# Narrower products for the diagonal key block in the two causal attentions of a hybrid decoder layer

## Chip, cores, metric

The kernel runs on one core of one Trainium2 chip. The metric is the device time of one execution in microseconds (us), the median of several runs. The engines are named as in the profile: PE (TensorE, products), PEld (its loads of the stationary operand, recorded apart), DVE (VectorE), ACT (ScalarE), POOL (GpSimd), SP (SyncE, which issues most transfers).

## What is computed

One decoder layer on 1024 tokens of width 1024: three mixers side by side (sparse attention A, latent attention B, cross-attention M into 256 memory tokens), each multiplied by a gate path, projected, merged by sigmoid gates and projected once more. What matters here are A and B, eight heads each, both causal over query blocks of 128:

```python
def one_block(args):                       # branch B; A is alike, with a top-k mask beside the causal one
    qb, start = args
    q_pos = start + jnp.arange(Q_BLOCK)    # Q_BLOCK = 128
    sc = jnp.einsum('bqhd,bkhd->bhqk', qb, k).astype(jnp.float32) * scale
    sc = jnp.where((key_pos[None, :] <= q_pos[:, None])[None, None], sc, NEG)
    p = jax.nn.softmax(sc, axis=-1).astype(v.dtype)
    return jnp.einsum('bhqk,bkhd->bqhd', p, v)
```

## The kernel before, in words

Every product of weight is made with float32r operands, a four-byte type that holds a rounded float32. To keep precision an operand is split in a high and a low part (names that end in h and l, as `b_3th` and `b_3tl`), and a product is two or three products of parts that add up in one bank of PSUM. Transposes go through PE as well, against an identity: `ident` for float32 data, `identr` for float32r data.

Both attentions run through the same function `attention`. Its work is cut into units of one head and one group G of two query blocks, 2G and 2G + 1, in the order G = 3, 0, 2, 1; there are 32 units in each branch. While the scores of one unit are made (`s_mm`, lines 997 to 999 in B with three products for each chunk of keys, 1481 and 1482 in A with two), the probabilities of the unit before it are multiplied with the values by class `PV`. For each pair of key blocks kp, `PV.pt` makes four transposes of 128x128 (line 466) into one bank, a cast by ACT to the high part (468) and a subtraction by DVE for the low part (469). `PV.mmv` then makes four products (479 and 480): values of key block 2kp against the high and the low part, and values of key block 2kp + 1 against both. Each streams 256 columns: the two query blocks side by side. `PV.evac` empties the result by ACT (487) and DVE (488).

The last pair, kp = G, holds the diagonal. Query block 2G sees nothing of key block 2G + 1, so only three of four 128x128 pieces are live. The kernel before keeps 256 columns there too: tiles `zt` hold zeros in their first quarter, written once by POOL at the start of each branch (441), and the other three quarters are filled by the casts. There are two pairs of such tiles in branch B (`ZTB`) and one in branch A. The other pairs use `pth` and `ptl` with two buffers each (`PVB`, `PVA`).

The first query block sees 128 keys, but `s_chunks` makes its scores 256 wide; the second half of the columns is not read.

Between these pieces stand products of other parts: the next pair of heads (`kv` in B, `a` in A) and the merge gates (`f`, class `Filler`), a few at a time by the counts in `PFB`, `PFA`, `GENB` and `GENA`. All of it is recorded in program order and then put into each engine's order by the framework's scheduler, which sees dependencies, buffers and pools. Where a size or a buffer changes, the order of rows on PE, ACT and DVE can change with it.

Of the kernel before, what the change touches and what calls it, by code (L numbers as in the profile page):

```python
# [73 lines left out]
ZTB = 2  # L74
PVB = (2, 2)
PVA = (2, 2)
# [28 lines left out]
def f(ap):  # L105
    return ap.bitcast(F32)
# [3 lines left out]
def hybrid_kernel(  # L110
# [32 lines left out]
    def ps_turn(nm, banks):  # L143
        """a bank of one of several kinds, in turn"""
        turn[0] += 1
        return banks[turn[0] % len(banks)](nm)

# [33 lines left out]
    # rotary tables: cos / sin of f32(position) * f32(inv_freq), by token block  # L181
# [40 lines left out]
    # DRAM scratch  # L222
# [30 lines left out]
    def wload(pool, nm, srcs, a, n):  # L253
        """srcs: list of ([128, a, w] DRAM view, w); -> (hi, lo) [P, a, n]"""
        def tile(dt, tag, bufs, nm):
            if len(pool_raw) < 3:
                return pool.tile([P, a, n], dt, tag=tag, name=nm, bufs=bufs)
            t = pool.tile([P, pool_raw[2]], dt, tag=tag, name=nm, bufs=bufs)
            return t[:, 0:a * n].rearrange("p (a n) -> p a n", a=a)
        raw = tile(F32, "raw", pool_raw[0], nm + "r")  # L260
        o = 0
        for ap, w in srcs:
            nc.sync.dma_start(raw[:, :, o:o + w], ap)
            o += w
        hi = tile(FR, "wp", pool_raw[1], nm + "h")
        lo = tile(FR, "wp", pool_raw[1], nm + "l")
        wsplit(hi, lo, raw)
        return hi, lo
# [12 lines left out]
    def proj_w(nm, pool, w, cols, nk, per=None):  # L281
        """cols: list of (c0, n) -> one (hi, lo) for each 128 rows"""
        tot = sum(n for _, n in cols)
        ks = []
        for kp in range(nk // 2):
            if per is not None:
                per(kp)
            hi, lo = wload(pool, f"{nm}w{kp}", [(wview(w, 2 * kp, 2, c0, n), n) for c0, n in cols], 2, tot)
            ks += [(hi[:, i, :], lo[:, i, :]) for i in range(2)]
        return ks  # L290

    def proj(nm, ks, lhs, tbs, chunks, consume):
        """out[tok, cols]; chunks: list of (off, n) within the columns"""
        nk = len(ks)
        for tb in tbs:
            for ci, (off, n) in enumerate(chunks):
                ps = ps_turn(f"{nm}ps{tb}_{ci}", pjb[0])
                for kt in range(nk):
                    ah, al = lhs(kt, tb)
                    wh, wl = ks[kt]  # L300
                    mm3(ps[:, 0:n], ah, al, wh[:, off:off + n], wl[:, off:off + n], kt == 0, kt == nk - 1)
                consume(tb, ci, ps)

# [15 lines left out]
    def row_factor(xp, xt, nm, r):  # L319
        """r <- rsqrt(mean square) of each row"""  # L320
        junk = xp.tile([P, D], BF, tag="junk", name=nm + "j", bufs=1)
        ss = sm.tile([P, 1], F32, tag="xss", name=nm + "ss")
        nc.scalar.activation(junk, xt, AF.Square, accum_out=ss)
        rsqrt_mean(r, ss, 1.0 / D)

    def norm_T(xp, xs, tbs, gcol, dst, nm, scale=True):
        """dst(k) -> (hi, lo) tiles [P, len(tbs) * 128]"""
# [16 lines left out]
    gates_done = set()  # L344

    class Filler:
        """tanh(gate / 2) of (branch, column block) jobs, a few products at a time"""
# [64 lines left out]
    def s_chunks(n):  # L412
        """(first key, width of the product, width used) of each bank"""
        if n <= 512:
            return [(0, max(n, 256), n)]
        if n == 640:
            return [(0, 384, 384), (384, 256, 256)]
        return [(0, 512, 512), (512, n - 512, n - 512)]
# [14 lines left out]
    zt = []  # L433
    zcount = [0]
    pv_bufs = [2, 2]

    def zero_tiles(wk, n):
        zt[:] = [[wk.tile([P, 4, P], FR, name=f"zt{i}{j}", bufs=1) for j in range(2)] for i in range(n)]
        for t2 in zt:
            for t in t2:  # L440
                nc.gpsimd.memset(t[:, 0, :].bitcast(F32), 0.0)

    class PV:
        """P of two query blocks (2G, 2G + 1) times V, transposed; vst(kt): [128, 128], high and low
        parts of V, the high part where the head's rows of the result lie."""
# [7 lines left out]
        def pt(self, kp):  # L453
            nm, wk, Pt = self.nm, self.wk, self.Pt
            tp = ps_t(f"{nm}pt{kp}").rearrange("p (a c) -> p a c", a=4)
            last = kp == self.nk - 1
            if last:
                th, tl = zt[zcount[0] % len(zt)]
                zcount[0] += 1
                order = [(1, 2 * kp + 1, 1), (2, 2 * kp, 0), (3, 2 * kp, 1)]  # L460
            else:
                th = wk.tile([P, 4, P], FR, tag="pth", name=f"{nm}th{kp}", bufs=pv_bufs[0])
                tl = wk.tile([P, 4, P], FR, tag="ptl", name=f"{nm}tl{kp}", bufs=pv_bufs[0])
                order = [(2 * a + b, 2 * kp + a, b) for a in range(2) for b in range(2)]
            for i, kt, b in order:
                nc.tensor.transpose(tp[:, i, :], Pt[b][:, kt * P:(kt + 1) * P], ident)
            v = slice(1 if last else 0, 4)
            nc.scalar.copy(th[:, v, :], tp[:, v, :])
            nc.vector.tensor_tensor(tl[:, v, :], tp[:, v, :], f(th[:, v, :]), op=ALU.subtract)
            kts = (2 * kp + 1, 2 * kp) if last else (2 * kp, 2 * kp + 1)  # L470
            self.t[kp] = (th.rearrange("p (a b) c -> p a (b c)", a=2), tl.rearrange("p (a b) c -> p a (b c)", a=2), kts)

        def mmv(self, kp):
            if self.o2 is None:
                self.o2 = ps_mm(f"{self.nm}o2")
            th, tl, kts = self.t.pop(kp)
            for a in range(2):
                vs = self.vst(kts[a])
                nc.tensor.matmul(self.o2[:, 0:256], vs, th[:, a], start=(kp == 0 and a == 0), stop=False)
                nc.tensor.matmul(self.o2[:, 0:256], vs, tl[:, a], start=False,  # L480
                                 stop=(kp == self.nk - 1 and a == 1))
# [10 lines left out]
    def masked(pt, sp, m, mask, k0, mx, c):  # L492
        """-(scores + mask), and its least value"""
# [40 lines left out]
    def attention(gen, k_prep, q_prep, scores, pv, fill, per, pre, GEN):  # L534
        """Head pairs; the next pair's operands are made between the units of this one."""
# [21 lines left out]
        def fl(k):  # L557
            """work of the next pair, then gate products"""
# [54 lines left out]
    # ================= memory branch =================  # L613
# [6 lines left out]
    with ExitStack() as ph:  # L620
# [31 lines left out]
        with ExitStack() as ph2:  # L652
# [44 lines left out]
            # the second half of h^T has no values yet: its tiles hold the weights of V  # L697
# [9 lines left out]
            # k_rope of branch B comes along with q_m  # L707
# [88 lines left out]
    # ================= branch B: latent attention =================  # L796
# [5 lines left out]
    def latent(nm, wpool, c0, nct, gofs, dst, wk, rb, rank, mid=None):  # L802
        """dst[ci] -> (hi, lo) [P, S]; what it returns sets rb to rsqrt(mean square) per token"""
# [19 lines left out]
        # three bfloat16 parts carry every bit of the sums  # L823
# [16 lines left out]
    with ExitStack() as ph:  # L840
        cb = ph.enter_context(tc.tile_pool(name="ckv", bufs=1, reuse_waits="tile"))
        ckv = [(cb.tile([P, S], FR, name=f"ckvh{i}"), cb.tile([P, S], FR, name=f"ckvl{i}")) for i in range(2)]
        with ExitStack() as ph2:
# [17 lines left out]
            # q_b = c_q w_uq: gain, rope; the norm's factor goes into the softmax scale  # L861
# [31 lines left out]
            # shared rotary key: sum of squares, gain, rotation  # L893
# [11 lines left out]
        zero_tiles(wk, ZTB)  # L905
# [118 lines left out]
    def topk_group(ts, nm, act):  # L1024
        """0 on the 256 largest of each row (the first ones among equals), NEG elsewhere: the bits of the
        256th largest value are found from the top by counting. VectorE counts values >= T. ScalarE sums
        the signs of x - T: (> T) - (< T), which may also settle on the number just below the 256th largest
        value when several values are equal to it; then the least value > T is the one."""
# [23 lines left out]
        # T has the low 16 bits all alike while its high half is sought: there the high halves of the values  # L1052
        # compare as the values do
# [5 lines left out]
        # on ScalarE T is kept negated  # L1059
# [19 lines left out]
        def sign(i, t):  # L1079
            """sign of x - T, and the number of positive ones"""  # L1080
# [51 lines left out]
    def both():  # L1132
        """steps of the two groups, TKR of VectorE's to one of ScalarE's"""
# [29 lines left out]
    if True:  # L1163
        pool_raw[:] = [2, 8]
        # ================= lightning indexer =================
# [74 lines left out]
    # ================= gates and branch projections =================  # L1240
    z_done = set()

    def z_part(n, w, zc, wpool, wk, zb=2, loaded=None):
        """2 silu(z) of 128 columns, by halves of the tokens"""
# [35 lines left out]
    def branch(n, zc, wpool, wk, yp, o_T, emit, bg=None, tgb=2, wkt=None, zb=2, ob=2, mid=None):  # L1280
        """emit(d, j, prod-writer) ; accumulates 4 * gate_n * branch_n transposed"""
# [86 lines left out]
    # ================= branch A: sparse attention =================  # L1368
    with w3s as ph:
# [17 lines left out]
        zero_tiles(wk2, 1)  # L1387
# [118 lines left out]
    # ================= branch A projection, merge, output projection =================  # L1506
# [91 lines left out]
```

## Time and profile before

| | us |
|---|---|
| median of 3 runs | 1428.13 |
| the runs | 1425.39 to 1431.31 |
| the profiled execution, its span | 1427.6 |

The profiled execution's own time is its span from the first to the last instruction; its runs lie around it on both sides, and the median is 0.5 us above it. In the rows below a line such as `L479` is a line of the kernel, `out<-in` are tile names with the numbers of buffers left out, and `128*128 128x256` means a stationary operand of 128x128 and 128 rows by 256 streamed columns. Starts in a timeline are rounded to 0.01 us. The recorded duration of a product holds its way through the array too, so consecutive records overlap; the pace is read from the starts.

### The profile page before, as it was taken

Reading aid. Unit: us, or ns where it says so; the run is one execution under the profiler, and the core shown is the slowest. Engines: PE = TensorE matmul, PEld = TensorE weight load, DVE = VectorE, ACT = ScalarE, POOL = GpSimd, SP = SyncE. Lnnn points to the kernel's source line nnn. Section 1 sums busy time; section 2 is a strip of 40 time slices with the busy share of each in tenths; the row PEclk is TensorE's granted clock in tenths of the full one; section 3 lists DMA queues with packets and bytes.
Section 4 is the critical chain, followed back from the end, with each engine's and each line's share of the span. In section 5 each row is a group of like instructions: output and inputs, shape, how many; then the busy total and the mean of one; then the engine's idle time right before and its main releaser. Section 6 shows DMA issues by size and latency. Waiting matters only on the chain.

```text
span 1427.6 us, 20798 instructions
## 1 busy us (share of the span) xinstructions
PE 1366.2 (96%) x7440; PEld 1173.0 (82%) x7440; DVE 967.5 (68%) x2409; ACT 687.7 (48%) x1488; POOL 270.2 (19%) x254
## 2 busy tenths in 40 slices
PE   7999999999999999898988998899999999999998
PEld 5998888888888889786867886689899898877887
DVE  5935446678888861479879678777777868836511
ACT  6635433356666651464576563224555535633200
POOL 3150003511102000200232335331202011003200
PEclk9999999999999999999998999999999999999999
DMA  7411222311111120210224325630201001185622
GB/s 245 136 45 52 78 59 86 114 56 41 49 56 53 45 93 20 67 45 23 89 79 151 97 75 182 193 85 9 67 23 45 31 15 45 38 276 184 210 96 74
DMA packets 124631, 122.34 MB, mean 86 GB/s; under 512 B 20336, under 2 KB 90224, under 8 KB 124528
## 3 DMA queue, kind: packets, MB, share of 16 engines
q1 hardware_dynamic: 123952, 118.92, 26.8%
q10 hardware_dynamic: 576, 2.10, 0.4%
q8 instruction: 58, 0.95, 0.3%
q14 instruction: 45, 0.37, 0.1%
HBM read 87.93 MB, written 33.06 MB: 85 GB/s over the span
## 4 chain that ended last, share of the span: by engine, by line
PE 68%; DVE 15%; ACT 6%; issue 4%; DMA 4%; POOL 1%; SPq 1%; ACTq 0%; DVEq 0%; POOLq 0%
PE f L277 5%; PE f L278 5%; PE f L279 4%; DVE kdj L1039 3%; PE a L277 3%; PE a L278 3%; PE a L279 3%; PE o L277 2%; PE o L278 2%; PE o L279 2%; ACT kag L1049 2%; PE br L277 2%; PE br L278 2%; PE br L279 2%; DVE sz L1292 1%
## 5 line engine op out<-in xcount | busy, mean ns | idle before, releaser
L1049 ACT ACTIVATE kag<-idx,kaT 128x512 bf16<-128x512 f32 (+2 forms) x96 | 82.9, 864 | 56.0 <-DVE kaT L1077 39.4
L277 PE MATMUL f<-hTh,f_0h 128*128 128x512 f32 x184 | 77.0, 419 | 1.9 <-ACT f_0h L248 1.2
L277 PE MATMUL f<-hTh,f_1h 128*128 128x512 f32 x184 | 75.6, 411 | 1.3 <-ACT f_1h L248 1.3
L279 PE MATMUL f<-hTh,f_0l 128*128 128x512 f32 x184 | 74.4, 405 | 0.6 <-POOL f_0l L251 0.6
L278 PE MATMUL f<-hTl,f_0h 128*128 128x512 f32 x184 | 74.5, 405 | 0.0
L279 PE MATMUL f<-hTh,f_1l 128*128 128x512 f32 x184 | 74.0, 402 | 0.0
L278 PE MATMUL f<-hTl,f_1h 128*128 128x512 f32 x184 | 73.6, 400 | 0.0
L1568 DVE TENSOR_TENSOR xr<-o,xr 128x512 f32<-128x512 f32 x16 | 11.1, 691 | 64.0 <-PE o L279 64.0
L1223 ACT ACTIVATE irl<-is 128x512 f32<-128x512 f32 (+1 forms) x80 | 37.6, 524 | 24.2 <-DVE idx L1229 15.5
L1526 POOL TENSOR_TENSOR ac<-ac,tg 128x512 f32<-128x512 f32 x16 | 23.5, 1469 | 128.6 <-DMA wo_3r<-in_w_out_dram 109.9
L1039 DVE TENSOR_SCALAR_CACHE_REDUCE kdj<-kdh,kdT 128x384 bf16<-128x384 bf16 (+2 forms) x48 | 46.3, 965 | 0.8
L1039 DVE TENSOR_SCALAR_CACHE_REDUCE kdj<-idx,kdT 128x384 bf16<-128x384 f32 (+2 forms) x48 | 46.2, 963 | 0.6
L369 ACT ACTIVATE fo<-f 128x512 f32<-128x512 f32 x48 | 28.7, 599 | 35.2 <-PE f L279 29.0
L279 PEld LDWEIGHTS f<-hTh,f_0l 128*128 128x128 f32 x184 | 35.2, 191 | 7.9 <-POOL f_0l L251 1.1
L1229 DVE SCALAR_TENSOR_TENSOR idx<-irl,wi,idx 128x1024 f32<-128x1024 f32 (+5 forms) x42 | 40.6, 966 | 1.5 <-ACT irl L1223 0.4
L277 PEld LDWEIGHTS f<-hTh,f_0h 128*128 128x128 f32 x184 | 35.1, 191 | 7.2 <-ACT f_0h L248 1.4
L279 PEld LDWEIGHTS f<-hTh,f_1l 128*128 128x128 f32 x184 | 34.8, 189 | 7.0 <-DVE f_1l L251 0.6
L277 PEld LDWEIGHTS f<-hTh,f_1h 128*128 128x128 f32 x184 | 35.0, 190 | 6.7 <-ACT f_1h L248 2.1
L278 PEld LDWEIGHTS f<-hTl,f_1h 128*128 128x128 f32 x184 | 34.9, 190 | 5.2
L278 PEld LDWEIGHTS f<-hTl,f_0h 128*128 128x128 f32 x184 | 35.3, 192 | 4.3
L1412 ACT ACTIVATE asq<-a 128x256 f32<-128x256 f32 x32 | 12.3, 384 | 51.1 <-PE a L279 50.9
L1266 DVE SCALAR_TENSOR_TENSOR sz<-sz,z 128x512 f32<-128x512 f32 x24 | 16.4, 683 | 27.7 <-ACT sz L1265 27.7
(1215 smaller groups left out, 4862.1 us busy)
## 6 DMA issues: line engine op xcount, KB each, us to landing
s_tg<-fo SPq DMA_DIRECT2D x48, 256.0 KB, 2.0
tg<-s_tg SPq DMA_DIRECT2D x48, 256.0 KB, 3.0
f_0r<-in_w_in_dram SPq DMA_DIRECT2D x23, 256.0 KB, 3.0
f_1r<-in_w_in_dram SPq DMA_DIRECT2D x23, 256.0 KB, 2.9
xx<-in_x_dram SPq DMA_DIRECT2D x8, 512.0 KB, 7.3
osb<-s_o SPq DMA_DIRECT2D x8, 512.0 KB, 3.8
s_acc<-acc SPq DMA_DIRECT2D x16, 256.0 KB, 2.4
ac<-s_acc SPq DMA_DIRECT2D x16, 256.0 KB, 3.4
```

The lines of the kernel that those rows point to most:

```text
L277: nc.tensor.matmul(ps, ah, bh, start=start, stop=False)
L278: nc.tensor.matmul(ps, ah, bl, start=False, stop=False)
L279: nc.tensor.matmul(ps, al, bh, start=False, stop=stop)
L369: nc.scalar.activation(o, ps, AF.Tanh, scale=0.5)
L1039: nc.vector.tensor_scalar(out=junk, in0=src[t], scalar1=T[:, i:i + 1], scalar2=0.0, op0=op, op1=ALU.add, accum_out=cnt[:, i:i + 1])
L1049: nc.scalar.activation(junk, idx[t], AF.Sign, bias=T[:, i:i + 1], accum_out=cnt[:, i:i + 1])
L1223: nc.scalar.activation(rl[:, k0:k0 + m], sp[:, 0:m], AF.Relu)
L1229: i_ = nc.vector.scalar_tensor_tensor(out=acc[:, 0:n], in0=rl[:, 0:n], scalar=wc, in1=acc[:, 0:n], op0=ALU.mult, op1=ALU.add)
L1266: zi[0] = nc.vector.scalar_tensor_tensor(out=sz, in0=sz, scalar=1.0, in1=pz[j], op0=ALU.add, op1=ALU.mult)
L1292: i_ = (nc.gpsimd if n and PMUL else nc.vector).tensor_tensor(sz, osb[:, cs], sz, op=ALU.mult)
L1412: nc.scalar.activation(sq.rearrange("p h d -> p (h d)"), ps[:, 0:256], AF.Square)
L1526: nc.gpsimd.tensor_tensor(ac, ac, tg, op=ALU.add)
```

## The change

The last pair of key blocks gets tiles of `pth` and `ptl` like the others, with the three live pieces side by side. The products with key block 2G keep 256 columns; those with key block 2G + 1 stream 128 columns into the second half of the result. The `zt` tiles and their memsets go, and `pth` and `ptl` get a third buffer. The scores of the first query block are 128 wide. The lines of comments that the diff also drops are left out here.

```diff
-ZTB = 2
-PVB = (2, 2)
-PVA = (2, 2)
+PVB = (3, 2)
+PVA = (3, 2)
...
     def s_chunks(n):
         if n <= 512:
-            return [(0, max(n, 256), n)]
+            return [(0, n, n)]
...
             last = kp == self.nk - 1
-            if last:
-                th, tl = zt[zcount[0] % len(zt)]
-                zcount[0] += 1
-                order = [(1, 2 * kp + 1, 1), (2, 2 * kp, 0), (3, 2 * kp, 1)]
-            else:
-                th = wk.tile([P, 4, P], FR, tag="pth", name=f"{nm}th{kp}", bufs=pv_bufs[0])
-                tl = wk.tile([P, 4, P], FR, tag="ptl", name=f"{nm}tl{kp}", bufs=pv_bufs[0])
-                order = [(2 * a + b, 2 * kp + a, b) for a in range(2) for b in range(2)]
-            for i, kt, b in order:
+            th = wk.tile([P, 4, P], FR, tag="pth", name=f"{nm}th{kp}", bufs=pv_bufs[0])
+            tl = wk.tile([P, 4, P], FR, tag="ptl", name=f"{nm}tl{kp}", bufs=pv_bufs[0])
+            order = [(2 * kp + a, b) for a in range(2) for b in range(2) if not (last and a > b)]
+            v = len(order)
+            for i, (kt, b) in enumerate(order):
                 nc.tensor.transpose(tp[:, i, :], Pt[b][:, kt * P:(kt + 1) * P], ident)
-            v = slice(1 if last else 0, 4)
...
         def mmv(self, kp):
...
             for a in range(2):
-                vs = self.vst(kts[a])
-                nc.tensor.matmul(self.o2[:, 0:256], vs, th[:, a], start=(kp == 0 and a == 0), stop=False)
-                nc.tensor.matmul(self.o2[:, 0:256], vs, tl[:, a], start=False,
-                                 stop=(kp == self.nk - 1 and a == 1))
+                vs = self.vst(2 * kp + a)
+                o = slice(P, 256) if last and a else slice(0, 256)
+                c = slice(256 * a, 256 * a + o.stop - o.start)
+                nc.tensor.matmul(self.o2[:, o], vs, th[:, c], start=(kp == 0 and a == 0), stop=False)
+                nc.tensor.matmul(self.o2[:, o], vs, tl[:, c], start=False, stop=bool(last and a))
...
-        zero_tiles(wk, ZTB)
...
-        zero_tiles(wk2, 1)
```

How the built order shows it, first on PE, at the end of the products of the first unit of branch B with its values (`b_3o` is that result, `b_2q` and `b_2S` belong to the next scores). Before:

```order
1643 L480 MATMUL b_3o_3228<-b_3tl_3221,vst_2885 128x256
1644 L479 MATMUL b_3o_3228<-b_3th_3220,vst_2885 128x256
1645 L480 MATMUL b_3o_3228<-b_3tl_3221,vst_2885 128x256
1646 L479 MATMUL b_3o_3228<-zt_2862,vst_2885 128x256
1647 L480 MATMUL b_3o_3228<-zt_2863,vst_2885 128x256
1648 L479 MATMUL b_3o_3228<-zt_2862,vst_2885 128x256
1649 L480 MATMUL b_3o_3228<-zt_2863,vst_2885 128x256
1650 L997 MATMUL b_2S_0_3273<-bkh_3009,b_2qh 128x384
```

The same place in the change, whose lines are some 11 to 13 lower:

```order
1639 L469 MATMUL b_3o_3220<-b_3tl_3213,vst_2877 128x256
1640 L966 MATMUL b_2q<-ident,xqp_2999 96x128 x2
1641 L468 MATMUL b_3o_3220<-b_3th_3226,vst_2877 128x256
1642 L469 MATMUL b_3o_3220<-b_3tl_3227,vst_2877 128x256
1643 L468 MATMUL b_3o_3220<-b_3th_3226,vst_2877 128x128
1644 L469 MATMUL b_3o_3220<-b_3tl_3227,vst_2877 128x128
1645 L984 MATMUL b_2S_0_3267<-bkh_3001,b_2qh 128x384
```

The number of products is the same, four; the last two are half as wide, and the first two no longer hold zeros. Rows of `kv` that stood ahead of them have moved behind.

On ACT, in branch A, where the probabilities of a unit with G = 3 are cast while the weights of the next pair of heads (`a3w0h`, `a3w1h`) are split. Before:

```order
994 L468 CAST a_3th_11768<-a_3pt_11767 128x512
995 L1418 CAST avst_11144<-a_6_11679 128x2x64
996 L248 CAST a3w0h<-a3w0r 128x768
997 L248 CAST a3w1h<-a3w1r 128x768
998 L468 CAST a_3th_11786<-a_3pt_11785 128x512
999 L468 CAST zt_9740<-a_3pt_11815 128x384
```

In the change:

```order
993 L455 CAST a_3th_11844<-a_3pt_11843 128x512
994 L501 ACTIVATE a_0p_11838,a_0rs<-a_0p_11838,a_0mx_11837 128x256
995 L1404 CAST avst_11212<-a_6_11755 128x2x64
996 L455 CAST a_3th_11862<-a_3pt_11861 128x512
997 L247 CAST a3w0h<-a3w0r 128x768
998 L247 CAST a3w1h<-a3w1r 128x768
999 L455 CAST a_3th_11892<-a_3pt_11891 128x384
```

The third cast, which has its own buffer now, stands ahead of the two casts of weights.

## Rows read from the trace of the kernel before

**Rows 1.** The page: span, and busy time of each engine.

```profile
span 1427.6 us, 20798 instructions
...
PE 1366.2 (96%) x7440; PEld 1173.0 (82%) x7440; DVE 967.5 (68%) x2409; ACT 687.7 (48%) x1488; POOL 270.2 (19%) x254
```

**Rows 2.** Busy time by stage, the columns named in the first line.

```profile
core 0: us, PE busy (x) PEld busy (x) DVE busy (x) ACT busy (x) POOL busy (x), PEclk, DMA share, GB/s
285.00:530.00 245.00, 241.70 (x1510) 210.33 (x1511) 198.59 (x582) 153.63 (x370) 25.58 (x29) 0.99 0.18 53
960.00:1250.00 290.00, 284.95 (x1745) 258.69 (x1746) 228.74 (x713) 153.49 (x364) 34.22 (x29) 0.99 0.12 35
```

**Rows 3.** What PE waited for, 285 to 530, then 960 to 1250, longest.

```profile
PE bkt L967 <- POOL xk L952: 2.4, 1, 2.4
...
PE akt L1449 <- DVE akd L1444: 2.9, 1, 2.9
```

**Rows 4.** Busy time by stage of instructions that touch `zt`.

```profile
285.00:530.00 245.00, 21.11 (x128) 19.09 (x128) 17.62 (x32) 15.42 (x32) 0.00 (x0) 0.99 0.18 53
960.00:1250.00 290.00, 22.39 (x128) 19.14 (x128) 17.58 (x32) 15.44 (x32) 0.00 (x0) 0.99 0.12 35
```

**Rows 5.** Readers of the first group's scores, `b_0S` and `a_0S`.

```profile
L494 DVE CUSTOM_DVE_ANT_0 b_0p<-b_0S,cmb x16: 273/351/420, 301.5 to 503.9; 128x128 f32<-128x128 f32 x8, 128x256 f32<-128x256 f32 x8
...
L494 DVE CUSTOM_DVE_ANT_0 a_0p<-a_0S,msk x16: 273/349/425, 973.2 to 1228.2; 128x128 f32<-128x128 f32 x8, 128x256 f32<-128x256 f32 x8
```

**Rows 6.** Timeline of PE, branch B: start us, us, engine, line, operation.

```profile
307.81 0.28 PE L479 MATMUL b_3o<-zt,vst 128*128 128x256 f32 x1
...
308.28 0.34 PE L997 MATMUL b_2S<-bkh,b_2qh 96*128 96x384 f32 x1
```

**Rows 7.** Timeline of PE, output projection: first and last of 22 rows.

```profile
1344.98 0.39 PE L277 MATMUL o<-wo_3h,hTh 128*128 128x512 f32 x1
...
1349.86 0.39 PE L277 MATMUL o<-wo_3h,hTh 128*128 128x512 f32 x1
```

**Rows 8.** Timeline of PEld, branch B: loads of the stationary operand.

```profile
307.34 0.19 PEld L480 LDWEIGHTS b_3o<-b_3tl,vst 128*128 128x128 f32 x1
307.45 0.19 PEld L479 LDWEIGHTS b_3o<-b_3th,vst 128*128 128x128 f32 x1
...
309.38 0.19 PEld L278 LDWEIGHTS kv<-ukv1l,ckvh 128*128 128x128 f32 x1
309.49 0.19 PEld L279 LDWEIGHTS kv<-ukv1h,ckvl 128*128 128x128 f32 x1
```

**Rows 9.** Timeline of PE, branch A, two transposes among products.

```profile
1057.49 0.29 PE L1465 MATMUL a_2q<-identr,a_2qs 128*128 128x128 f32 x2
1057.61 0.35 PE L479 MATMUL a_3o<-zt,avst 128*128 128x256 f32 x1
1057.80 0.28 PE L480 MATMUL a_3o<-zt,avst 128*128 128x256 f32 x1
```

**Rows 10.** Timeline of PE: transposes of float32r (`identr`), then of float32 (`ident`).

```profile
622.68 0.80 PE L1210 MATMUL iqt<-identr,iqs 128*128 128x128 f32 x8
623.32 0.47 PE L277 MATMUL f<-hTh,f_0h 128*128 128x512 f32 x1
...
971.03 0.28 PE L1465 MATMUL a_0q<-identr,a_0qs 128*128 128x128 f32 x2
971.15 0.40 PE L279 MATMUL a<-a1w2h,hTl 128*128 128x384 f32 x1
...
1118.40 0.95 PE L466 MATMUL a_1pt<-ident,a_1p 128*128 128x128 f32 x7
1119.11 0.48 PE L278 MATMUL f<-hTl,f_1h 128*128 128x512 f32 x1
```

**Rows 11.** Waits around `a_3th`, 960 to 1250: total us, times, (longest).

```profile
ACT a_3th L468 <- PE a_3o L479: 7.4, 7, 3.1
...
PEld a_3o L479 <- ACT a_3th L468: 0.6, 2, 0.4
```

**Rows 12.** The memsets of `zt` on POOL.

```profile
L441 POOL MEMSET zt<- 128x128 f32 x6 | 1.0, 198 | 0.0
```

More of the change, by code (lines that the diff above doesn't have):

```diff
@@ L431, in rope @@
         nc.vector.tensor_tensor(x2, tt[2], tt[3], op=ALU.add)
-    zt = []
-    zcount = [0]
     pv_bufs = [2, 2]
[L437 to L441, printed above, removed]
     class PV:
@@ L456, in pt @@
             last = kp == self.nk - 1
-            if last:
-                th, tl = zt[zcount[0] % len(zt)]
-                zcount[0] += 1
-                order = [(1, 2 * kp + 1, 1), (2, 2 * kp, 0), (3, 2 * kp, 1)]
-            else:
-                th = wk.tile([P, 4, P], FR, tag="pth", name=f"{nm}th{kp}", bufs=pv_bufs[0])
-                tl = wk.tile([P, 4, P], FR, tag="ptl", name=f"{nm}tl{kp}", bufs=pv_bufs[0])
-                order = [(2 * a + b, 2 * kp + a, b) for a in range(2) for b in range(2)]
-            for i, kt, b in order:
-                nc.tensor.transpose(tp[:, i, :], Pt[b][:, kt * P:(kt + 1) * P], ident)
-            v = slice(1 if last else 0, 4)
[L468 to L471, printed above, removed]
+            th = wk.tile([P, 4, P], FR, tag="pth", name=f"{nm}th{kp}", bufs=pv_bufs[0])
[3 more added lines that the diff above has]
+            for i, (kt, b) in enumerate(order):
+                nc.tensor.transpose(tp[:, i, :], Pt[b][:, kt * P:(kt + 1) * P], ident)
+            nc.scalar.copy(th[:, 0:v, :], tp[:, 0:v, :])
+            nc.vector.tensor_tensor(tl[:, 0:v, :], tp[:, 0:v, :], f(th[:, 0:v, :]), op=ALU.subtract)
+            self.t[kp] = (th.rearrange("p i c -> p (i c)"), tl.rearrange("p i c -> p (i c)"))
         def mmv(self, kp):
@@ L475, in mmv @@
                 self.o2 = ps_mm(f"{self.nm}o2")
-            th, tl, kts = self.t.pop(kp)
+            th, tl = self.t.pop(kp)
+            last = kp == self.nk - 1
             for a in range(2):
-                vs = self.vst(kts[a])
-                nc.tensor.matmul(self.o2[:, 0:256], vs, th[:, a], start=(kp == 0 and a == 0), stop=False)
-                nc.tensor.matmul(self.o2[:, 0:256], vs, tl[:, a], start=False,
-                                 stop=(kp == self.nk - 1 and a == 1))
+                vs = self.vst(2 * kp + a)
[3 more added lines that the diff above has]
+                nc.tensor.matmul(self.o2[:, o], vs, tl[:, c], start=False, stop=bool(last and a))
         def evac(self):
```

## Prediction

> **What bounds the kernel now.** I read the page first, then the busy times of the two stages that the change touches, then what PE waits for in them, and last the timelines of PE and of its loads, because the question is what one product costs there.
>
> The page gives a span of 1427.6 us, of which PE is busy 1366.2 [rows 1]. That share is an average, and busy records overlap, so it proves little by itself. The stages say more. Branch B fills 285 to 530 us and branch A 960 to 1250 us; PE is busy 241.70 of 245 us and 284.95 of 290 us, at a granted clock of 0.99 in both, which is the 2.4 GHz level with little lost. DVE comes next with 198.59 and 228.74 us, or 81% and 79% [rows 2]. The waits of PE are few: the longest is one of 2.4 us in B and one of 2.9 us in A, each at the hand-over to other heads, not at the products that change [rows 3]. So in these stages the time is set by the pace at which PE takes instructions, and what a product gives up in pace comes off the span nearly in full. The other engines have room for a stage a few us shorter.
>
> **The pace of a product.** Four products with `zt` start from 307.81, and the product after them at 308.28: 0.47 / 4 = 0.1175 us for 256 columns [rows 6]. With 512 columns, 21 steps take 1349.86 - 1344.98 = 4.88 us, or 0.2324 us each [rows 7]. The difference is 0.1149 us for 256 columns, so a line through both leaves 0.1175 - 0.1149 = 0.003 us at zero columns: from 256 columns up the pace follows the columns. What it does below is not in this trace. No float32r product narrower than 256 columns stands there, and whether the line goes on to 128 is the whole question.
>
> **How many products change.** `zt` is used by 128 products in each branch [rows 4]; half of these, those of the second key block, become 128 wide: 64 + 64 = 128. Of the 16 score blocks of the first group in each branch, 8 belong to the first query block (the reader of 128 columns) and 8 to the second [rows 5]. The first become narrow, with three products each in B and two in A: 24 + 16 = 40. Together 168 products go from 256 to 128 columns. The number of products, transposes, casts and subtractions stays as it is.
>
> **What one narrow product gains.** Every product has a load of its own: 7440 of one and of the other [rows 1]. The load for the next product runs while this one streams. Two loads of float32r values are never closer in the rows shown than 307.34 to 307.45 and 309.38 to 309.49: 0.11 us [rows 8]. In the first of these the loads catch up after a pause, so the step shows what a load itself takes. A product of 256 columns hides that (0.1175 against 0.11). One of 128 columns does not: if its streaming takes half, the next product still waits for its own load. So I expect 0.11 us in place of 0.1175, a gain of 0.0075 us. The narrow work that the trace does have speaks for this. Two float32r transposes of 128 columns start at 1057.49, the next product is recorded at 1057.61, but the one after it only at 1057.80, which is 0.19 us for 256 columns in place of 0.12 [rows 9]: the product behind narrow work waits, and the pair cost (0.31 - 0.1175) / 2 = 0.096 us each, not the 0.06 that their own starts seem to say.
>
> The bounds. Above: 971.03 to 971.15 for two transposes, 0.06 us each [rows 10], a gain of 0.0575 us. Between: 0.096 us, a gain of 0.0215. Below: no gain. In all, 168 x 0.0075 = 1.3 us, with 0 to 3.6 us as the bounds from the rows nearest to it (a product behind narrow work), and 168 x 0.0575 = 9.7 us as the far one. I take 1.3, since the loads are of the same kind as those of the changed products, while those of the transposes may be shorter.
>
> The Trainium skill, "TensorE: Matmul & The Clock Gate", section "LDWEIGHTS (loading the stationary operand)", speaks against the change in the same way: a load takes the number of stationary columns over 1.2 GHz, whatever the number of rows, which for 128 columns is an estimate of 107 ns. The trace agrees (0.11 us); by that figure the sum would be 168 x (117.5 - 107) = 1.8 us in place of 1.3.
>
> **The third buffer.** ACT waited 7.4 us in 7 places in branch A for products with an earlier `a_3th` before it could cast the third one; PE's loads in turn waited 0.6 us for such a cast [rows 11]. With three buffers that cast goes ahead of two casts of weights, as the order shows. The last pair now shares these buffers, but its tile was read by products that stand ahead of its transposes in the program, so I expect no wait in exchange. PE gains between 0 and 0.6 us; I take 0.6. Most of the 7.4 us is idle time of an engine that is busy about half of the stage [rows 2], and costs nothing.
>
> **The rest at nothing.** Six memsets on POOL go, 1.0 us [rows 12]; POOL is busy 19% [rows 1], and nothing in the waits above ends on them. Their cover is the start of each branch; without it they would cost at most the 1.0 us. The live pieces are as many as before, so casts and subtractions keep their width of 384. The new order of PE's rows moves whole groups of `kv` and `f` products by a few places. They cost what they cost; what may change is PE's idle time, which is 245 - 241.70 = 3.3 us in B and 290 - 284.95 = 5.05 us in A [rows 2]. It could shrink or grow by a part of that; I take 0, with 3 us to each side.
>
> **Sum.** 1427.6 - 1.3 - 0.6 = 1425.7 us for an execution like the profiled one. The median of the runs is 0.5 us above that execution's time, so the forecast is 1426.2, as a round number 1426 us. Faster by 0.13%, which cannot be told from no change: the runs of one kernel spread over 6 us, and about 0.5%, or 7 us, is what a measurement can tell.
>
> **Rivals.**
>
> *The columns decide after all* (faster). If a narrow product is paced like the transposes, it takes 0.06 us at best (gain 9.7 us, 1418 us in all with the buffer), or as in the run of eight from 622.68 to 623.32, 0.64 / 8 = 0.08 us (gain 168 x 0.0375 = 6.3 us, 1421 us) [rows 10]. For it: these are float32r data of 128 columns with a load for each. Against it: the 0.11 us between loads of products [rows 8] and the product that is late behind the pair [rows 9]. The same page of the Trainium skill has a rule that would decide so: section "Back-to-back issue gap" gives some 81 ns for each pair of load and product of 128 columns, sustained; by that estimate the gain would be 168 x (117.5 - 81) = 6.1 us. The run of eight transposes agrees with it (0.08 us); no row shows it for products.
>
> *A narrow float32r product is slower than a wide one* (slower). If a product of fewer than 256 float32r columns doesn't run as one pass, but as float32 would, in several, its pace rises. The price at four passes is that of 4 x 128 = 512 columns: 0.2324 - 0.1175 = 0.1149 us each, 168 x 0.1149 = 19.3 us, or 1446 us with the buffer's gain. It decides the sign as soon as a narrow product takes more than 0.1175 us, and can be measured above 0.1175 + 7.1 / 168 = 0.160 us. For it: every float32r product in the trace has 256 columns or more, so no row excludes it, and four-byte types do differ: float32 transposes take (1119.11 - 1118.40) / 7 = 0.10 us where float32r ones take 0.06 to 0.08 [rows 10]. Against it: the float32r transposes of that width pay no such price. The Trainium skill, "FP8 and Floating Point Precision", section "TensorE Precision Notes", tells of four passes for true float32 only, with the reduced type as a truncated read; no run here shows a product of either kind at 128 columns.
>
> *The order costs more than the products give* (no change or slower). The scheduler's new order lets PE wait where it didn't, most likely at `akt` and `bkt`, whose waits of 2.9 and 2.4 us are the longest now [rows 3]. If both double, 5.3 us are lost and the time is 1426 + 5 = 1431.
>
> **Chances and range.** The forecast (pace set by the load) 0.61; paced by columns 0.14; several passes 0.18; order 0.07. The likeliest's own range is 1422 to 1430: 3.6 us of gain at most and 3 us of order, and the spread of runs. The whole range reaches down to the columns' 1418 and up past the order's 1431 to a partial price of narrow products, 1437; it leaves out the full four passes, and little else. Faster by over 0.5% (below 1421) needs the columns' case nearly in full or a better order on top: 0.15. Slower by over 0.5% (above 1435) is the several passes, and a small part of the order: 0.20. Within 0.5%: 0.65.
>
> **What the new profile would show.** If I am right: products with 128 columns start some 0.11 us apart and their loads are as close as 0.11; branches B and A together are 1 to 3 us shorter; the wait of ACT for `a_3o` before `a_3th` is gone. If the columns decide, narrow products start 0.06 to 0.08 apart. If several passes, the starts after a narrow product lie 0.2 us apart or more. What would make me wrong without any of these: a PE wait of several us that isn't in the trace now, at the start of a pair of heads.

## The result: slower by 1%, and the profile after

| | us |
|---|---|
| after, median of 4 runs | 1442.78 (1442.16 to 1443.68) |
| before, median of 4 runs beside them | 1428.12 (1425.39 to 1431.31) |
| ratio, 95% interval | 1.0103 (1.0088 to 1.0118) |

The forecast was 1426 us, with 1418 to 1437 as the range. The kernel became 14.7 us slower and lies outside it. From the page of the changed kernel, span and busy times:

```profile
span 1440.4 us, 20809 instructions
...
PE 1368.1 (95%) x7440; PEld 1171.2 (81%) x7440; DVE 969.0 (67%) x2409; ACT 686.7 (48%) x1488; POOL 269.1 (19%) x248
```

Against [rows 1] the span grows by 12.8 us and PE's busy time by 1.9, so PE stands still more often, or waits inside a record. To see in which stage, four rows of PE's timeline serve as marks: the first scores of branch B, the first product behind B, the first scores of branch A, and A's last product with its values. In the kernel before, then in the changed one:

```profile
294.88 0.40 PE L997 MATMUL b_3S<-bkh,b_3qh 96*128 96x512 f32 x1
...
533.71 0.31 PE L277 MATMUL ixps<-ixw0h,hTh 128*128 128x320 f32 x1
...
965.60 0.48 PE L1481 MATMUL a_3S<-akh,a_3qT 128*128 128x512 f32 x1
...
1249.47 0.28 PE L480 MATMUL a_1o<-zt,avst 128*128 128x256 f32 x1
```

```profile
294.84 0.40 PE L984 MATMUL b_3S<-bkh,b_3qh 96*128 96x512 f32 x1
...
538.69 0.31 PE L276 MATMUL ixps<-ixw0h,hTh 128*128 128x320 f32 x1
...
970.84 0.48 PE L1467 MATMUL a_3S<-akh,a_3qT 128*128 128x512 f32 x1
...
1263.15 0.27 PE L469 MATMUL a_1o<-a_1tl,avst 128*128 128x128 f32 x1
```

B takes 538.69 - 294.84 = 243.85 us and A 1263.15 - 970.84 = 292.31. In the kernel before B took 238.83 and A 283.87. B lost 5.0 us and A 8.4; all the rest together won 0.6. These two lengths, B and A, are given for every experiment below, each from one profiled execution; experiments 1 and 7, which differ in little else than columns, agree within 0.03 and 0.24 us.

What PE waits for in 285 to 540 us and then in 955 to 1270 us (total us, times, longest). Before the change, beside [rows 3]:

```profile
PE b_2pt L466 <- DVE b_2p L523: 0.2, 1, 0.2
...
PE a_2S L1481 <- DVE a_2mx L494: 0.3, 1, 0.3
```

After it:

```profile
PE bkt L954 <- POOL xk L939: 2.4, 1, 2.4
PE b_3pt L454 <- DVE b_3p L511: 1.6, 6, 0.3
PE b_2pt L454 <- DVE b_2p L511: 1.4, 3, 0.6
...
PE a_2S L1467 <- DVE a_2mx L482: 3.6, 2, 2.9
PE akt L1435 <- DVE akd L1430: 2.6, 1, 2.6
PE f L276 <- ACT fo L368: 1.8, 1, 1.8
```

`bkt` and `akt` wait about as before. What has grown are transposes that wait for DVE's normalised probabilities, and scores that wait until DVE has masked the scores in their bank (`a_2mx`). A wait that ends inside PE's modelled records is seen better at the loads. The same stretches for PEld, before the change:

```profile
PEld b_3S L997 <- DVE b_3mx L494: 1.3, 4, 0.4
...
PEld b_3pt L466 <- DVE b_3p L523: 0.9, 4, 0.2
...
PEld b_2pt L466 <- DVE b_2p L523: 0.8, 3, 0.3
...
PEld a_2S L1481 <- DVE a_2mx L494: 2.0, 6, 0.5
```

and after it:

```profile
PEld b_2pt L454 <- DVE b_2p L511: 3.4, 7, 1.0
PEld b_3pt L454 <- DVE b_3p L511: 2.7, 6, 0.5
...
PEld b_3S L984 <- DVE b_3mx L482: 2.1, 6, 0.6
...
PEld a_2S L1467 <- DVE a_2mx L482: 6.4, 10, 3.2
...
PEld f L276 <- ACT fo L368: 2.5, 2, 2.3
```

All rows of this view add up to 14.7 us before (22 rows) and 19.6 after (19) in B, and to 17.2 (20) and 25.2 (21) in A: 4.9 and 8.0 us more, nearly the 5.0 and 8.4 that the stages lost.

Most of these waits are of half a microsecond or less. One is long enough to be followed through three engines. DVE, POOL and PE of the changed kernel, branch A, head 5 (timelines; in brackets the idle time before the row and what ended it):

```profile
1193.37 0.22 DVE L430 TENSOR_TENSOR axk<-ar_0rp,ar_0rp 128x64 f32<-128x64 f32 x1
1196.36 0.22 DVE L425 TENSOR_TENSOR ar_1rp<-axq,cos_a 128x64 f32<-128x64 f32 x1 [2.78 <-POOL axq L1416]
1196.51 0.55 DVE L482 CUSTOM_DVE_ANT_0 a_2p<-a_2S,msk 128x384 f32<-128x384 f32 x1
```

```profile
1192.01 2.90 POOL L240 TENSOR_TENSOR arr<-arr,mhalf 128x16 f32<-128x16 f32 x1
...
1195.28 1.05 POOL L1416 TENSOR_TENSOR axq<-axq,arr 128x512 f32<-128x512 f32 x1
```

```profile
1193.08 0.34 PE L1468 MATMUL a_2S<-akl,a_2qT 128*128 128x384 f32 x1
...
1197.12 0.50 PE L1467 MATMUL a_2S<-akh,a_2qT 128*128 128x512 f32 x1 [2.91 <-DVE a_2mx L482]
```

The scores were there at 1193.4 and DVE was free from 1193.59 on. But its next row was a rotary product of operands for the next heads, whose input POOL finished only at 1196.33. The mask stood behind that row, and PE behind the mask. In the kernel before, the four masks of `a_2S` stand ahead of this rotary product (masks from 1184.31 to 1187.12 us, the product at 1187.47).

### The profile page after: what moved, and what is told of

It reads as the page before. It is cut to its first block, busy times and chain, and to the rows that moved or that the text cites. A ratio compares the mean times of both kernels' runs of the same rounds, so it can differ in the third digit from the quotient of the medians.

```text
span 1440.4 us, 20809 instructions
## 1 busy us (share of the span) xinstructions
PE 1368.1 (95%) x7440; PEld 1171.2 (81%) x7440; DVE 969.0 (67%) x2409; ACT 686.7 (48%) x1488; POOL 269.1 (19%) x248
## 4 chain that ended last, share of the span: by engine, by line
PE 67%; DVE 16%; ACT 7%; issue 4%; DMA 3%; POOL 1%; SPq 0%; ACTq 0%; DVEq 0%; POOLq 0%
PE f L276 5%; PE f L277 4%; PE f L278 4%; DVE kdj L1026 3%; PE a L276 3%; PE a L277 3%; PE a L278 3%; PE o L277 2%; PE o L276 2%; PE o L278 2%; PE br L276 2%; PE br L278 2%; PE br L277 2%; ACT kag L1036 2%; DVE sz L1279 1%
## 5 line engine op out<-in xcount | busy, mean ns | idle before, releaser
L1398 ACT ACTIVATE asq<-a 128x256 f32<-128x256 f32 x32 | 12.3, 385 | 56.1 <-PE a L278 56.0
```

What stands on the lines that cost most here:

```text
L1398: nc.scalar.activation(sq.rearrange("p h d -> p (h d)"), ps[:, 0:256], AF.Square)
```

## Experiments

Theory O: a narrow product is paced by its load, as forecast, and the time goes into the new order of rows. Theory W: the 128-column products themselves cost it. Theory S: the shared buffers that replaced the tiles of zeros cost it.

The framework picks each engine's order. To hold it fixed, a list of places was added, and each instruction made to depend on the one ahead of it in the list, without a semaphore:

```diff
     with _tile.TileContext(nc) as tc:
         hybrid_kernel(tc, *args)
+        pin_order(tc, _ORD)
...
+def pin_order(tc, ords):
+    info = mybir.DependencyInfo(mybir.DependencyClass.NoSync, mybir.DependencyReason.DATA)
...
+            tc.add_manual_dep(mine[k + d[k]], mine[k - 1 + d[k - 1]].name, info, reason="order")
```

This works because both programs have 7440 instructions on PE, 1223 on ACT, 2109 on DVE and 427 transfers on SP, one for one. The orders differ in 1654, 220, 377 and 15 places. Where an edit below says "pinned", this is meant. One engine alone can't be pinned to the other order: with PE in one order and DVE and ACT in the other they would wait for each other in a circle. So what each engine's order costs by itself was not tried.

Experiments 1 to 4, 5 to 8 and 9 to 12 ran on three chips, each with the kernel before beside them: 1429.32, 1428.73 and 1429.69 us. The ratios are to these; between the groups ratios compare better than microseconds.

**1. The changed kernel, pinned to the order of before.**

> The changed program with its narrow products and its three shared buffers, but PE, ACT, DVE and SP each issue their instructions in the order of the kernel before (the k-th of one program in the place of the k-th of the other). Theory O, that the order of the rows costs the time and a narrow product is paced by its own load: 168 x 0.0075 us less than before, so about 1427 us, inside 1424 to 1430, with PE busy in the stretches of attention no longer than before. Theory W, that the 128-column products cost it wherever they stand: 1440 us or more. Theory S, that the last block's tiles in the shared buffers cost it: 1435 to 1443 us, with new waits of PE's transposes and of ACT's copies for buffers.

Measured: 1430.52 us, ratio 1.001 (1.0000 to 1.0019); B 241.32, A 284.55. Of the 14.7 us only 1.2 remain. That is 0.5 us above O's range, which ended at 1430, and far from W's 1440: W falls. S is not quite dead: B is still 2.5 us longer than before, with a new wait, taken up in experiment 8.

**2. The kernel before, pinned to the order of the changed one.**

> The kernel before with its 256-column products and its tiles of zeros, but PE, ACT, DVE and SP each issue their instructions in the order of the changed kernel. Theory O: as slow as the changed kernel, 1440 to 1446 us, with PE waiting for DVE's b_3p before the transposes b_3pt as after the change. Theory W: no slower than before, 1426 to 1430 us. Theory S: 1426 to 1430 us too, since the last blocks keep buffers of their own.

Measured: 1453.89 us, ratio 1.0175 (1.0160 to 1.0190); B 245.48, A 304.41. The order makes the old products slow as well, and in A by 12 us more than the changed kernel, which O did not say. Waits of ACT, then of PE, in A:

```profile
ACT a_3th L468 <- PE a_3o L479: 14.2, 7, 3.1
...
PE a_2S L1481 <- DVE a_2mx L494: 11.0, 3, 4.2
```

With two buffers ACT's cast waits 14.2 us for products to let go of one, where it was 7.4 in the old order [rows 11], and DVE's masks come later still. With each of PE's three waits for `a_2mx` (4.15, 3.98 and 2.88 us) the granted clock also fell to 0.50, the 1.2 GHz level, for a few us; the last section comes back to this. So in this order the third buffer is needed; experiment 10 measures the same order with it.

**3. The kernel before with narrow scores only.**

```diff
-            return [(0, max(n, 256), n)]
+            return [(0, n, n)]
```

> The kernel before, only the 40 score products of the first query block are 128 wide. The framework then moves 916 of PE's 7440 rows and 165 of DVE's 2109. Theory O: the time follows the order, which no price of a product gives: 1425 to 1440 us, and whatever is lost stands as waits of PE for DVE in the attention of B or A. Theory W: 40 of 168 parts of the 14.7 us lost, so about 1431.6 us. Theory S: 1427 to 1429 us, as no buffer changes.

Measured: 1433.16 us, ratio 1.0031 (1.0020 to 1.0041); B 242.29, A 285.83. Forty narrow products, no other buffer, and B loses 3.5 us: its loads wait 2.9 us for `b_2p` and 2.7 for `b_3p`, as after the full change. W's number (1431.6) is near, so this run does not tell O from W; S is excluded as the only cause.

**4. The changed kernel with wide scores.** (The edit of 3 in reverse.)

> The changed kernel with the scores of the first query block left 256 wide, so only its 128 narrow products with the values, its shared buffers and no tiles of zeros. PE's order is near to that of the changed kernel (475 rows differ) and far from before's (1540 differ). Theory O: most of the loss stays, 1434 to 1444 us. Theory W: 128 of 168 parts of the 14.7 us, so about 1439 us. Theory S: 1440 to 1443 us. This run tells how the loss is shared out between the two narrow kinds, not O from W.

Measured: 1443.84 us, ratio 1.0101 (1.0080 to 1.0122); B 244.28, A 293.23: the whole loss. The two narrow kinds don't share it out: 3.8 us and 14.5 us alone, 14.7 together.

**5. The changed kernel, pinned to its own order, one row of DVE moved.** Places 1880 to 1888 of DVE's list:

```diff
-L425 ar3_7_1rp0 <- axq3, cos_a
 L482 a5_2p0 <- a5_2S0_0 (mask)
...
 L482 a5_2p1 <- a5_2S1_1 (mask)
+L425 ar3_7_1rp0 <- axq3, cos_a
 L426 ar3_7_1rp1 <- axq3, sin_a
```

> The changed kernel in its own order on PE, ACT, DVE and SP, but one row of DVE moved: in the third of branch A's head pairs that make operands ahead, the first rotary product of the queries (ar_1rp from axq, L425), which waits 2.86 us for POOL's axq, stands behind the four masks of a_2S and no longer ahead of them. PE waits 2.9 us there for a_2mx. Theory O with its mechanism (a row that waits on DVE holds up ready rows behind it, and PE with them): this wait goes and the kernel takes 2 to 3 us less than the changed one, 1439.5 to 1441 us. Rival: the wait comes back at DVE's next rows or PE's, 1442 to 1443 us.

Measured: 1439.59 us, ratio 1.0080 (1.0066 to 1.0093); B 243.96, A 288.98, 3.3 us less than the changed kernel's A. PE's wait for the masks in A:

```profile
PE a_2S L1467 <- DVE a_2mx L482: 0.8, 2, 0.6
```

It was 3.6 us. From the product `f` ahead of these scores to the scores it took 3.38 us in the changed kernel (1193.74 to 1197.12) and takes 0.37 here, 3.0 us of the 3.3. One row of 2109 that waited in the wrong place is worth 3 us; this shows the mechanism by itself. The other 11 us or so of the loss were not taken apart row by row: for them there are the exchange of whole orders and the lists of waits.

**6. The changed kernel with two buffers, its order left to the framework.**

```diff
-PVB = (3, 2)
-PVA = (3, 2)
+PVB = (2, 2)
+PVA = (2, 2)
```

> The changed kernel with two shared buffers in both branches in place of three, in the order that the framework then chooses (667 of PE's rows differ from the changed kernel's, 1672 from the order before). Theory S (buffers set the loss): slower than the changed kernel, 1446 us or more, with ACT's copies of the transposes waiting for PE's products to let go of a buffer. Theory O: the order that it happens to get decides, anything from 1432 to 1448 us, and the waits of PE for DVE account for it.

Measured: 1442.56 us, ratio 1.0100 (1.0086 to 1.0114); B 243.99, A 293.04. The same time as with three. ACT does wait for buffers in A (7.2 us for `a_2o`, 6.3 for `a_3o`), but the framework laid out the rows around that, and PE's waits for DVE's `b_2p` (1.6 us) and `b_3p` (1.3) stay. S in its strong form falls.

**7. As 1, with 64 columns in the 128 narrow products with values.**

```diff
-                o = slice(P, 256) if last and a else slice(0, 256)
+                o = slice(P, P + 64) if last and a else slice(0, 256)
```

> As the first of these kernels (narrow products in the order of the kernel before), but the 128 narrow products with the values stream 64 columns and not 128: half of the second query block's last key block is left out of the sum. If a narrow product is paced by its own weight load: no change against that kernel, 1429.5 to 1431.5 us. If it is paced by its columns: 128 x 64 columns at 2.4 GHz = 3.4 us less, about 1427 us.

Measured: 1430.47 us, ratio 1.0008 (0.9999 to 1.0018), against 1430.52 and 1.0010 in experiment 1; B 241.35, A 284.31. Columns below 128 give nothing that can be told: 3.4 us would be 0.0024 of the ratio, and 0.0002 are there. The same place as [rows 6] shows why. PE with 128 columns (experiment 1), then with 64, then PEld with 64:

```profile
306.66 0.22 PE L468 MATMUL b_3o<-b_3th,vst 128*128 128x128 f32 x1
306.72 0.28 PE L469 MATMUL b_3o<-b_3tl,vst 128*128 128x128 f32 x1
306.84 0.39 PE L984 MATMUL b_2S<-bkh,b_2qh 96*128 96x384 f32 x1
307.06 0.34 PE L985 MATMUL b_2S<-bkl,b_2qh 96*128 96x384 f32 x1
```

```profile
305.53 0.20 PE L468 MATMUL b_3o<-b_3th,vst 128*128 128x64 f32 x1
305.56 0.28 PE L469 MATMUL b_3o<-b_3tl,vst 128*128 128x64 f32 x1
305.67 0.42 PE L984 MATMUL b_2S<-bkh,b_2qh 96*128 96x384 f32 x1
305.93 0.34 PE L985 MATMUL b_2S<-bkl,b_2qh 96*128 96x384 f32 x1
```

```profile
305.41 0.19 PEld L468 LDWEIGHTS b_3o<-b_3th,vst 128*128 128x128 f32 x1
305.53 0.19 PEld L469 LDWEIGHTS b_3o<-b_3tl,vst 128*128 128x128 f32 x1
305.64 0.19 PEld L984 LDWEIGHTS b_2S<-bkh,b_2qh 96*128 96x128 f32 x1
305.75 0.19 PEld L985 LDWEIGHTS b_2S<-bkl,b_2qh 96*128 96x128 f32 x1
```

The second product of a pair starts after 0.06 us or 0.03, but the loads follow each other by 0.11 to 0.12 us at either width, and the two wide products behind pay for it. From the first product of the pair to the second one of `b_2S` it is 0.40 us with 128 columns and 0.40 with 64; with 256 columns it was 0.42 (308.04 to 308.46). A narrow pair gives back 0.02 us.

**8. As 1, with four shared buffers in B** (`PVB = (4, 2)`), as many as two and two tiles of zeros made before.

> As the first of these kernels (narrow products in the order of the kernel before), with four shared buffers in branch B in place of three, as many as the kernel before has there with its two tiles of zeros. In the first of these kernels PE waits 2.7 us in branch B for DVE's ob before products of kv, and ahead of that ACT's copy b_2th starts only when the products b_0o have let go of a buffer. If the third buffer's sharing makes these waits: they go, 1427 to 1428.5 us, 0.1% less than before. If they come from the narrow products' own timing: 1430 to 1431 us.

Measured: 1428.22 us, ratio 0.9997 (0.9988 to 1.0005); B 238.13, A 284.41. Experiment 1 had these waits in B, of which this run has neither:

```profile
ACT b_2th L455 <- PE b_0o L468: 4.0, 3, 1.5
...
PE kv L276 <- DVE ob L476: 2.7, 3, 1.2
```

Three buffers are one too few for the old order. With four, B is 0.7 us shorter than before the change. Spread over its 88 narrow products that is 0.008 us each, near the forecast's 0.0075.

**9. The changed kernel with all 168 products wide, its order left to the framework.**

```diff
-            return [(0, n, n)]
+            return [(0, max(n, 256), n)]
...
-                o = slice(P, 256) if last and a else slice(0, 256)
-                c = slice(256 * a, 256 * a + o.stop - o.start)
+                o = slice(0, 256)
+                c = slice(P, 384) if last and a else slice(256 * a, 256 * a + 256)
```

> The changed kernel with its three buffers and without tiles of zeros, but all 168 products 256 wide again: the scores of the first block as before, and the last key block's products stream the 256 columns beside it, with one block of the wrong probabilities in the place of the zeros. The framework chooses the order, and lays out PE's rows near to the kernel before (622 rows differ; 1548 from the changed kernel). Theory O with the widths as what makes the framework choose: 1428 to 1433 us. Rival, that the shared buffers and the lost tiles of zeros make the loss: 1440 us or more.

Measured: 1429.02 us, ratio 0.9996 (0.9987 to 1.0005); B 239.81, A 284.98. In the order that the framework gives this program, the shared buffers and the lost tiles of zeros cost nothing in the median; in the profiled execution its B and A together are 2.1 us longer than before, so a small cost there is not excluded. In the old order three buffers did cost (experiments 1 and 8). As soon as the products are 256 wide the framework goes back to nearly the old order, and the time goes with it.

**10. The same program, pinned to the order of the changed kernel.**

> The same program with all 168 products 256 wide (one block of wrong probabilities in the place of the zeros), but PE, ACT, DVE and SP in the order of the changed kernel. It tells how much the width itself is worth in that order, free of the kernel before's buffers, with which it took 1453.9 us. Narrow products worth their loads' 0.0075 us each: 1.3 us over the changed kernel, 1443 to 1445 us; then it was buffers that cost 10 us in the earlier run. Width worth more in that order, because it delays what waits: 1448 to 1454 us.

Measured: 1442.09 us, ratio 1.0092 (1.0078 to 1.0106); B 244.43, A 292.68, that is 0.6 and 0.4 us more than the changed kernel. The medians say 0.7 less and the ratios 0.0011 less, with intervals that overlap, so the width cannot be told from nothing in this order. The 12 us more of experiment 2 go with its buffers: PE waits 4.0 us for `a_2mx` here, not 11.0, and no cast `a_3th` of ACT waits for a product `a_3o`.

**11. As 8, with 21 ready rows of PE moved ahead of two waiting transposes:** 11 products `f` ahead of the first `bkt`; four products `a` and six `f` ahead of the second `akt`.

> Narrow products, four shared buffers in branch B, the order of the kernel before, and 21 of PE's rows moved ahead of two transposes that wait: 11 filler products f ahead of the first bkt (PE waits 2.4 us there for POOL's xk), and 4 products a and 6 f ahead of the second akt (2.7 us, DVE's akd). If a waiting row costs what stands ready behind it: both waits shrink by 2.4 and 2.0 us, 1424 to 1426 us, under both kernels. Rival: the moved rows were cover where they stood, and the waits come back there: 1427.5 to 1429 us.

Measured: 1424.95 us, ratio 0.9971 (0.9959 to 0.9982), the fastest of all; B 238.03, A 284.27. PE's waits, B then A:

```profile
PE bkt L954 <- DVE xk L939: 1.7, 1, 1.7
...
PE a L277 <- POOL a1w3l L250: 1.5, 1, 1.5
...
PE akt L1435 <- DVE akl L1438: 0.7, 1, 0.7
```

In B the wait goes from the first `bkt`, and one of 1.7 us comes up at the next, where the moved rows had been cover. Still the stretch from the first `kv` to the first `ixps` falls from 257.36 us in experiment 8 to 255.06. Only part of this is the moved rows. In the profiled execution of experiment 8 the granted clock fell behind the wait (0.76, then 0.50 in 288 to 292 us); in this one it stayed at 1.00. From the first `kv` to the first `b_3S` it took 19.23 us there and 17.03 here, and 17.74 in experiment 1, which has the wait and a clock of 1.00: so 0.7 us are the rows and 1.5 the clock. In A it is half a failure: the four moved `a` need weights that POOL had not split yet.

**12. The kernel before, pinned, with the same 21 rows moved.**

> The kernel before, 256-column products and tiles of zeros, with the same 21 rows of PE moved ahead. If the order alone brings the gain of the run before this one, this one stands 0.4 to 1.3 us over it, 1424.5 to 1427 us, and the narrow products are worth no more than that; if the narrow products make the gain, this one stays at 1428 to 1429 us.

Measured: 1427.92 us, ratio 0.9988 (0.9979 to 0.9997); B 238.82, A 284.90. The order alone gives 1.8 us (1429.69 beside it). It is 3.0 us over the run before it, more than the 1.3 allowed. B and A account for 0.8 + 0.6 of that. In the profiled executions most of the rest lies between the first `akt` and the first `a_3S`, 13.71 us against 12.16: behind a wait for weights (`a1w3l`, 1.7 and 1.5 us) the granted clock fell to 0.50 here (960 to 962 us) and stayed at 1.00 in experiment 11. So the 3.0 us are not shown to be the narrow products' doing; whether the clock falls there in the other runs is not known.

## Why the prediction was wrong

**The step that failed** is the term for the new order: "The new order of PE's rows moves whole groups of `kv` and `f` products by a few places. They cost what they cost; [...] I take 0, with 3 us to each side." It was mis-sized. Measured, it is 12 to 15 us: 1442.78 - 1430.52 = 12.3 with the changed program under the two orders (experiment 1), 1442.09 - 1429.02 = 13.1 with wide products (experiments 10 and 9), and 1442.78 - 1428.22 = 14.6 against experiment 8, which has one buffer more. The bound came from PE's idle time in the two stages, 3.3 and 5.05 us [rows 2]. But idle time that exists is no measure of idle time that can be made, and the step looked at PE's rows alone, where 377 rows of DVE had moved too.

**The rival of the order** was right in kind and got 0.07. Its place was wrong: it named `akt` and `bkt`, which stayed at 2.6 and 2.4 us, where many small waits for `b_2p`, `b_3p` and `a_2mx` came. So was its price, 5 us. The sign named for being wrong in another way, a new wait of PE of several us, came once, 2.91 us in A, in the middle of a head and not at the start of a pair. The row that made it, worth 3 us (experiment 5), stood in the built order before anything ran: a product that needs POOL's `axq`, ahead of masks that need only PE.

**The price of a narrow product** is borne out in B: paced by its load at 0.11 us, a gain of 0.0075 us each. For the 88 in B that is 0.66 us; three pairs of kernels that share an order give 0.7 (before and 8), 0.8 (12 and 11) and 0.6 (10 and the changed one). In A the last two pairs give 0.6 and 0.4 for 80 products, the first -0.5. By medians it cannot be told from nothing. The forecast's sign, starts 0.11 us apart, shows in the loads and not in the starts of the products.

**Paced by columns**: not borne out. Starts 0.06 us apart do occur, which was that rival's sign, but only inside a pair, and the product behind gives the time back, as [rows 9] had suggested. The page "TensorE: Matmul & The Clock Gate" of the Trainium skill puts a load at an estimated 107 ns for 128 columns ("LDWEIGHTS (loading the stationary operand)"); the loads here follow by 0.11 to 0.12 us, in agreement. Its 81 ns for a pair of load and product ("Back-to-back issue gap") was not reached by these products at 128 columns, nor at 64.

**Several passes**: not borne out. The median happens to lie near its 1446 us, but 0.40 us for a place that took 0.42 leaves no room for 0.1149 us more on each product.

**The third buffer** (0.6 us of gain): ACT's wait for `a_3o` before `a_3th`, 7.4 us before, is gone from the changed kernel, as foreseen. Whether that gave 0.6 us cannot be told: experiment 9 lies 0.7 us below the kernel before, with an interval from 1.9 us below to 0.7 above. Its reason "I expect no wait in exchange" fails in the old order, where sharing three buffers cost B 3.2 us (241.32 against 238.13, experiments 1 and 8).

**The memsets** at nothing: experiment 9 has none, and its gain cannot be told from nothing either.

That the widths made the framework choose another order is shown (9 against the changed kernel); that it does so because its own estimate of a product's time follows the columns is only argued.

## What to carry to other kernels

Where a scheduler lays out the engines' rows, a change of a size is two changes, and the second can be ten times the first: compare the built orders on every engine, and look for a row that waits for a slow engine and has moved ahead of ready rows that others need. To measure the two apart, hold the order fixed and change the size, then the reverse. And before columns are cut, look at the spacing of the loads: what is below it is not given back.

## Unexpected of the hardware

A wait of PE can cost more than its length. Behind the 2.4 us at the first `bkt` the granted clock (third figure from the end) was at its lower level, 0.50 or 1.2 GHz, for a while in the profiled execution of the kernel before; busy time by stretch:

```profile
288.00:290.00 2.00, 2.00 (x8) 1.54 (x7) 1.12 (x3) 1.10 (x3) 1.26 (x1) 0.68 0.36 124
290.00:292.00 2.00, 2.00 (x6) 1.62 (x5) 1.70 (x4) 0.62 (x1) 0.00 (x0) 0.50 0.00 0
```

In experiment 1, with the same wait of 2.4 us, it was 1.00 in both stretches, and PE issued 24 products there in place of 14. From the first `bkt` to the first `b_3S` it took 7.56 us in the one (287.32 to 294.88) and 6.01 in the other (287.74 to 293.75), so 1.5 us hang on it. Twelve of the fourteen kernels have this wait, and in their profiled executions the clock fell behind it in six (the kernel before, the changed one, experiments 4, 6, 8 and 10) and not in the other six. The marks of B begin behind this place and are free of it.

In A the clock fell during or right behind every one of the six waits of 2.9 us or more (2.88 to 4.15) for `a_2mx`: one each in the changed kernel and in experiments 4 and 10, three in experiment 2. In the changed kernel, behind the wait that ends at 1197.12:

```profile
1199.00:1201.00 2.00, 2.00 (x7) 1.71 (x7) 2.00 (x12) 1.93 (x5) 0.00 (x0) 0.50 0.35 131
1201.00:1203.00 2.00, 2.00 (x8) 1.62 (x8) 1.91 (x6) 0.68 (x3) 0.00 (x0) 0.75 0.00 0
```

It cost little there: from these scores to the next `a_2pt` it took 6.61 us, and 6.27 in experiment 5, where the wait is gone and the clock stayed at 1.00 but PE waited elsewhere. What decides whether the clock falls stays open.
